# The entry of a two-layer transformer block: other banks, row buffers, matmul order and load order for the last modulation quarters

## The chip, the core and the metric

The kernel runs on one core of one Trainium2 chip. The core has five engines that run side by side and meet only through semaphores: TensorE (PE in the profile, its weight loads PEld), VectorE (DVE), ScalarE (ACT), GpSimd (POOL) and SyncE (SP), which here only issues DMAs. The time is the device time of one execution in microseconds (us), lower is better. Before the change it was 1694.29 us, the median of three executions (1693.81, 1694.29 and 1697.91).

## The reference

Layer 0 begins with an RMS norm of 512 latent and 256 context tokens, a scale and a shift of each of the 1024 features that come from a conditioning vector ("modulation"), and a projection into queries, keys and values. Only this entry is touched by the change.

```python
s_c, s_cc = silu(c), silu(c_ctx)
mx = s_c @ mod_w[l] + mod_b[l]              # 6*1024 values: shift, scale, gate, twice
shx1, scx1, gx1, shx2, scx2, gx2 = split(mx, 6)
hx = rms(x, norm_mix_w[l]) * (1.0 + scx1) + shx1
hc = rms(ctx, norm_mix_w[l]) * (1.0 + scc1) + shc1   # the same with s_cc
ax, ac = even_mixer(hx, hc, ev_w_in, ...)   # q, k, v = h @ ev_w_in, then attention
```

What follows (attention, output projection, a SwiGLU feed-forward, and layer 1 with differential attention) makes up most of the time and is unchanged.

## The kernel before

**Tiling.** All tokens stand in six tiles of 128: 4 and 5 are context, 0 to 3 latent. They are taken in the order 4, 5, 0, 1, 2, 3 (`CTX_FIRST`). The 1024 features are eight slices k = 0 to 7 of 128. The normalised tokens are turned (transposed) by PE into `xT`, features on the partitions (lines 1161 to 1172); `modulated(k)` (line 1182) then scales and shifts slice k on DVE, casts it on ACT into a high part and subtracts on DVE (latent) or POOL (context) into a low part. The tiles of these parts are hT0, hT1 for latent and hTc0, hTc1 for context tokens.

**Modulation.** Shift (part 0) and scale (part 1) are made in four quarters n = 0 to 3 of 256 features. Quarter n serves the slices k = 2n and 2n+1. One quarter of one part is a run of `mod_steps` (line 168):

- two loads of 512 KB each (line 177, tile `modw`, "pieces" in what follows), and for each piece four matmuls into a PSUM tile `mod` (line 182). The trace counts each fp32 matmul twice, so a piece is "x8" there;
- a copy on ACT into the row buffer `modr` (line 185);
- two small matmuls `modcol` that bring the row into columns (line 191), in a PSUM bank that is named by the argument `bank`;
- `add_mod` on DVE: `modc` (line 276), and for the scale also `aff` (line 280).

Quarters 0, 1 and 2 ran to their end in `start_mod` (line 1152), with `mod` in the wide score buffers (pool `p_sc`) and `modcol` in the banks acc0 (shift) and acc1 (scale). Quarter 3 was `late` (line 1174), and its `mod` itself was in acc0 and acc1. There was one row buffer `modr` for all of them.

**Weights.** `weights0` (line 481) brings the first head group's projection weights in four units of 384 KB (tile `wir`, three loads each, line 491), casts each on ACT to `wihi` (line 498) and subtracts on DVE to `wilo` (line 499). The unit u serves the slices 2u and 2u+1. All four were loaded behind the pieces of quarter 3. Pieces and weights of the start share six buffers of one tag (`start_tile`, line 1149), in turn; so a load waits until the matmuls have read what its buffer held. The two shift pieces of quarter 3 lie elsewhere (`raw_tile`).

**Order.** A scheduler places the instructions of each engine by its own estimate, and every engine runs its list in order: an instruction that waits holds up all that stand behind it. From line 1175 on PE's list is given by the order of the code (`manual_schedule`); other matmuls, those of the latent tokens above all, are filled in between by the scheduler. The projections are `inps` (line 465): tokens 4, 5, 0 and 1 collect in two wide score buffers, token 2 in acc0 and token 3 in acc1; 24 matmuls each. SP's list is one queue for all loads. `behind(name)` makes the scheduler place what is inside it after the instruction remembered under that name.

Of the kernel before, what the change touches and what calls it, by code (L numbers as in the profile page):

```python
# [63 lines left out]
def backbone(es: ExitStack, tc: tile.TileContext, x, c, ctx, c_ctx, mod_w, mod_b, norm_mix_w, norm_ffn_w,  # L64
# [3 lines left out]
    nc = tc.nc  # L68
# [7 lines left out]
    p_sc = None  # L76
    turn = {"acc": 0, "tr": 0, "sum": 0}
# [29 lines left out]
    @contextmanager  # L107
    def behind(*names):

        with ExitStack() as st:  # L110
            for name in names:
                if name in turn:
                    st.enter_context(tc.issue_after(turn[name].ins))
            yield

    def f32(ap):
        return ap.bitcast(F32)
# [4 lines left out]
    start = Pool("start")  # L122
# [45 lines left out]
    def mod_steps(l, part, n, new_tile, pool, bank, wide=None, room=("modr", 1)):  # L168

        width, pieces = 256, 2  # L170
        c0 = part * D + n * width
        ps = p_1.tile([P, width], F32, name="mod", tag=bank) if wide is None else \
            wide.pool.tile([P, 1024], F32, name="mod", tag="sc", bufs=2)[:, :width]
        kp = KT // pieces
        for pc in range(pieces):
            w = new_tile([P, kp, width], "modw")
            nc.sync.dma_start(
                w, mod_w[l, pc * kp * P:(pc + 1) * kp * P, c0:c0 + width].rearrange("(j p) n -> p j n", p=P))
            for a in range(kp):
                k = pc * kp + a  # L180
                j = k % 4
                nc.tensor.matmul(ps[32 * j:32 * j + 32, :], s_pad[:, k, :], w[:, a, :],
                                 start=k < 4, stop=k >= 4, tile_position=(0, 32 * j))
        r = pool.tile([P, width], F32, name="modr", tag=room[0], bufs=room[1])
        turn["modr"] = nc.scalar.copy(r, ps)
        yield
        nb = width // P
        k0, k1 = n * nb, (n + 1) * nb
        pc2 = p_1.tile([P, nb, 2], F32, name="modcol", tag=bank)
        for b in range(nb):  # L190
            nc.tensor.matmul(pc2[:, b, :], r[:, b * P:(b + 1) * P], sel2, start=True, stop=True)
        add_mod(l, part, k0, k1, pc2, 2)

    def mod_chunk(*args, **kw):
        for _ in mod_steps(*args, **kw):
            pass

    def mod_stream(groups, pool, bank):
# [74 lines left out]
    def add_mod(l, part, k0, k1, ps, streams):  # L273

        mc = modc[l][:, part, k0:k1, 0:streams]
        nc.vector.tensor_tensor(mc, ps, bc(bcol[:, l, part, k0:k1], 2, streams), ALU.add)
        if part in (1, 4):
            f = 0 if part == 1 else 1
            w0 = 16 + 16 * f + 8 * l
            nc.vector.scalar_tensor_tensor(aff[l][:, f, k0:k1, 0:streams], mc, 1.0,  # L280
                                           bc(cols[:, w0 + k0:w0 + k1], 2, streams), ALU.add, ALU.mult)
# [24 lines left out]
    def ctx_room(shape, dtype, name):  # L306

        return [keep.tile(shape, dtype, name=f"{name}{j}", tag=f"hTc{j}") for j in range(2)]
# [7 lines left out]
    def cols_T(j, s0, s1):  # L316

        return hT[j][0][:, :, s0:s1] if s1 <= SEQ else hT[j][1][:, :, s0 - SEQ:s1 - SEQ]
# [162 lines left out]
    def weights0(b, wp, subs, new_tile=raw_tile, loads=((0, 1), (), (2,), (3,))):  # L481

        qc, kc, vc = ((b * 256, 512 + 64 * b, 640 + 64 * b) if b < 2 else
                      (768 + (b - 2) * 256, 1280 + 64 * (b - 2), 1408 + 64 * (b - 2)))
        for u in range(4):
            if not u:
                raws = []
            for v in loads[u]:
                raws.append(new_tile([P, 2, 384], "wir"))
                for c0, c1, s in ((0, 256, qc), (256, 320, kc), (320, 384, vc)):  # L490
                    turn["load"] = nc.sync.dma_start(
                        raws[-1][:, :, c0:c1],
                        ev_w_in[0, v * 256:(v + 1) * 256, s:s + c1 - c0].rearrange("(j p) n -> p j n", p=P))
            if not u:
                yield
            raw = raws.pop(0)
            hi, lo = (wp.tile([P, 2, 384], F32R, name=f"wi{z}", tag=f"w{z}", bufs=WBUF + 1) for z in ("hi", "lo"))
            nc.scalar.copy(hi, raw)
            subs[u % len(subs)].tensor_sub(lo, raw, f32(hi))
            yield hi, lo  # L500
# [264 lines left out]
    def out_units0(wp):  # L765
        def tile(name, dtype):
            return wp.tile([P, D], dtype, name=name, tag="w", bufs=2 * KT)

        raws = [tile("wor", F32) if k < KT - 2 else raw_tile([P, D], "wor") for k in range(KT)]
        for k, raw in enumerate(raws):  # L770
            nc.sync.dma_start(raw, ev_w_out[0, k * P:(k + 1) * P, :])
        for raw in raws:
            hi, lo = tile("woh", F32R), tile("wol", F32R)
            nc.scalar.copy(hi, raw)
            nc.vector.tensor_sub(lo, raw, f32(hi))
            yield hi, lo
# [375 lines left out]
    def start_mod(n):  # L1152
        for part in range(2):
            mod_chunk(0, part, n, start_tile, start.pool, f"acc{part}", p_sc)

    p_sc = Pool("p_sc0", space=PSUM)
    wp = Pool("mw0", "right")
# [5 lines left out]
    for t in CTX_FIRST:  # L1163
# [4 lines left out]
        for g in range(2):  # L1168
# [1 line left out]
            for k in range(4):  # L1170
                nc.tensor.transpose(pt[:, k, :], h[:, (4 * g + k) * P:(4 * g + k + 1) * P], ident)
            nc.scalar.copy(xT[:, 4 * g:4 * g + 4, t * P:(t + 1) * P], pt)
    start_mod(2)
    late = [mod_steps(0, part, 3, (raw_tile, start_tile)[part], start.pool, f"acc{part}") for part in range(2)]
    manual = tc.manual_schedule(engines={mybir.EngineType.PE})
    manual.__enter__()
    for g in late:
        next(g)
    units = weights0(0, wp.pool, (nc.vector,), start_tile, ((0, 1, 2, 3), (), (), ()))
    next(units)  # L1180

    def modulated(k):
        for i, (s0, s1) in ((1, (SEQ, TOK)), (0, (0, SEQ))):
            nc.vector.tensor_scalar(xT[:, k, s0:s1], xT[:, k, s0:s1], aff[0][:, 0, k, i:i + 1],
                                    modc[0][:, 0, k, i:i + 1], ALU.mult, ALU.add)
        for s0, s1, ks in ((SEQ, TOK, slice(k - 1, k + 1)), (0, SEQ, slice(k, k + 1))):
            if s0 == 0 or k % 2:
                hi, lo = (cols_T(j, s0, s1)[:, ks, :] for j in range(2))
                turn["started"] = nc.scalar.copy(hi, xT[:, ks, s0:s1])
                (nc.gpsimd if s0 else nc.vector).tensor_sub(lo, xT[:, ks, s0:s1], f32(hi))  # L1190

    ws, begun, first = [], {}, CTX_FIRST[:2]
    for k in range(6):
        modulated(k)
        if k % 2:
            ws += islice(units, 1)
    for i in range(0, 4, 2):
# [88 lines left out]
    units = weights0(1, wp.pool, (nc.gpsimd, nc.vector))  # L1286
# [3 lines left out]
    if True:  # L1290
        for i, (b, t) in enumerate(steps):
# [8 lines left out]
            if j == 4 and b < 2:  # L1300
                units = weights0(b + 2, wp.pool, (nc.gpsimd, nc.vector))
# [28 lines left out]
            if t == 0:  # L1330
# [13 lines left out]
                wp = Pool("w0", "right")  # L1344
                opa = Pool("opa", "right")
                xs = [None] * NT
                units = out_units0(wp.pool)
# [17 lines left out]
            else:  # L1365
# [8 lines left out]
                if t == 4:  # L1374
                    room = [z[:, 0] for z in ctx_room([P, 1, KT, P], F32, "nroom")]
# [185 lines left out]
    p_sc = Pool("p_sc1", space=PSUM)  # L1561
    fp = out0
    mods1.close()
    wp = Pool("mw1", "right")
# [7 lines left out]
    late = []  # L1572
# [36 lines left out]
    if True:  # L1609
# [117 lines left out]
        wp = Pool("w1", "right")  # L1727
# [146 lines left out]
    p_sc = None  # L1874
# [56 lines left out]
```

## Time and profile before

| what | value |
|---|---|
| time, median of three | 1694.29 us |
| time, lowest and highest | 1693.81, 1697.91 us |
| span of the profiled execution, first to last instruction | 1695.6 us |
| PE busy | 1631.5 us, 96% of the span |
| DVE, ACT, POOL busy | 1146.7, 937.0, 696.4 us |
| mean granted TensorE clock | 0.992 |

The timed values are those of the three executions; of the profiled one the page tells the span, 1.3 us above the median. Times "at 42.91" are counted from the span's start. A row of a timeline gives the start, the length, the engine, the line, what it writes and reads, the count, and in brackets how long the engine had been idle and what released it. The entry of layer 0 are the first 45 of the 1695.6 us.

### The profile page before, as it was taken

How to read it: one execution, taken by the hardware profiler on the slowest of the kernel's cores; microseconds unless marked ns; L12 is line 12 of the kernel's file. 1: busy time of each engine (PE TensorE's matmuls, PEld its weight loads, DVE VectorE, ACT ScalarE, POOL GpSimd, SP SyncE). 2: the span in 40 equal slices, each digit the busy share in tenths (PEclk: the TensorE clock that was granted, in tenths of full speed). 3: DMA queues.
4: the chain of work that ended last, by engine and by line, in shares of the span. 5: the costliest groups of instructions: out<-in, count | busy, mean ns of one | idle time of the engine just before them, and what ended most of it. 6: DMA issues, size and time to landing. Idle time of an engine off the chain costs nothing. (4 is left out here: it accounts for less than half of the span.)

```text
span 1695.6 us, 28585 instructions
## 1 busy us (share of the span) xinstructions
PE 1631.5 (96%) x10390; PEld 1468.6 (87%) x10390; DVE 1146.7 (68%) x2014; ACT 937.0 (55%) x2011; POOL 696.4 (41%) x867
## 2 busy tenths in 40 slices
PE   6999999899999999999999989999999999999998
PEld 3977787677999999998777889999988899999887
DVE  3765656754799887767767656666666598887434
ACT  5565555745456665545554456666666555555320
POOL 2665554321346554412413366666664242221000
PEclk8999999999999999999999999999999999999999
DMA  9222221411455555439966311111112433331431
GB/s 319 69 71 74 70 70 50 164 60 38 129 167 172 164 159 162 134 108 347 296 184 189 99 43 38 48 42 44 50 45 97 125 93 102 111 101 57 137 99 62
DMA packets 218108, 194.64 MB, mean 115 GB/s; under 512 B 20016, under 2 KB 202864, under 8 KB 217968
## 3 DMA queue, kind: packets, MB, share of 16 engines
q1 hardware_dynamic: 217616, 192.62, 36.8%
q8 instruction: 81, 1.33, 0.3%
q14 instruction: 59, 0.48, 0.1%
q10 hardware_dynamic: 352, 0.21, 0.0%
HBM read 179.92 MB, written 12.87 MB: 114 GB/s over the span
## 5 line engine op out<-in xcount | busy, mean ns | idle before, releaser
L901 ACT CAST wbh<-wr 128x512 fp32r<-128x512 f32 x170 | 104.9, 621 | 130.2 <-PE p L933 73.4
L933 PE MATMUL p<-hT,wbh 128*128 128x256 f32 (+1 forms) x752 | 154.5, 299 | 0.0
L465 PE MATMUL inps<-wih,hT 128*128 128x384 f32 x512 | 144.2, 344 | 7.3 <-ACT qkv L677 7.3
L911 POOL TENSOR_TENSOR wbl<-wr,wbh 128x512 fp32r<-128x512 f32 x43 | 60.0, 1396 | 173.6 <-ACT wbh L901 173.6
L933 PEld LDWEIGHTS p<-hT,wbh 128*128 128x128 f32 x752 | 121.9, 191 | 0.2
L911 DVE TENSOR_TENSOR wbl<-wr,wbh 128x512 fp32r<-128x512 f32 x127 | 107.7, 858 | 21.0 <-ACT wbh L901 16.8
L933 PE MATMUL p<-hT,wbl 128*128 128x256 f32 (+1 forms) x376 | 111.9, 298 | 0.0
L933 PE MATMUL p<-t,wbh 128*128 128x384 f32 (+1 forms) x480 | 111.3, 318 | 0.0
L604 POOL TENSOR_SCALAR Pt<-Pt,rc 128x256 f32<-128x256 f32 (+3 forms) x96 | 74.6, 788 | 89.3 <-DVE rc L601 83.1
L231 POOL TENSOR_TENSOR modp<-modp 128x512 f32<-128x512 f32 x40 | 57.4, 1436 | 114.3 <-ACT modp L230 114.3
L465 PEld LDWEIGHTS inps<-wih,hT 128*128 128x128 f32 x512 | 93.3, 188 | 10.6 <-ACT qkv L677 9.7
L933 PE MATMUL p<-hTt,wbh 128*128 128x256 f32 (+1 forms) x480 | 101.0, 302 | 0.0
L887 POOL TENSOR_TENSOR wr<-wr 128x512 f32<-128x512 f32 x40 | 61.6, 1540 | 89.8 <-DVE ws L892 85.8
L933 PE MATMUL p<-b,wbh 128*128 128x384 f32 x368 | 93.8, 336 | 0.2 <-DVE c L961 0.2
L901 ACT CAST wbh<-ws 128x512 fp32r<-128x512 f32 x120 | 69.4, 579 | 43.1 <-PE p L933 29.0
L224 DVE SCALAR_TENSOR_TENSOR ma<-modw,cols,ma 128x256 f32<-128x256 f32 x140 | 89.2, 637 | 2.3
L592 ACT ACTIVATE Pt<-sc,nm 128x256 f32<-128x256 f32 (+3 forms) x96 | 67.6, 707 | 35.3 <-DVE nm L588 16.9
L465 PE MATMUL inps<-wil,hT 128*128 128x384 f32 x256 | 86.0, 336 | 0.0
L933 PEld LDWEIGHTS p<-t,wbh 128*128 128x128 f32 x480 | 82.9, 189 | 0.0
L911 DVE TENSOR_TENSOR wbl<-ws,wbh 128x512 fp32r<-128x512 f32 x120 | 81.7, 681 | 1.7 <-ACT wbh L901 1.6
L933 PEld LDWEIGHTS p<-hTt,wbh 128*128 128x128 f32 x480 | 78.3, 191 | 3.1 <-ACT modp L230 1.6
L230 ACT ACTIVATE modp<-modw,cols 128x256 f32<-128x256 f32 x160 | 68.4, 500 | 18.0 <-POOL ma L236 10.1
(355 smaller groups left out, 5217.9 us busy)
## 6 DMA issues: line engine op xcount, KB each, us to landing
modw<-in_mod_w_dram SPq DMA_DIRECT2D x96, 512.0 KB, 5.2
wr<-in_ffn_w_in_dram SPq DMA_DIRECT2D x176, 256.0 KB, 2.9
wdr<-in_ffn_w_out_dram SPq DMA_DIRECT2D x66, 512.0 KB, 3.7
wir<-in_od_w_in_dram SPq DMA_DIRECT2D x96, 128.0 KB, 2.3
hidm<-hid SPq DMA_DIRECT2D x44, 192.0 KB, 1.9
hr<-hidm SPq DMA_DIRECT2D x22, 192.0 KB, 3.5
x<-in_x_dram SPq DMA_DIRECT2D x8, 512.0 KB, 3.5
wir<-in_ev_w_in_dram SPq DMA_DIRECT2D x16, 256.0 KB, 3.5
```

The costliest lines, as they stand in the source:

```text
L224: nc.vector.scalar_tensor_tensor(acc, w[:, k], scale[k], acc, ALU.mult, ALU.add)
L230: nc.scalar.activation(pr[:, k], w[:, k], AF.Copy, scale=scale[k])
L231: nc.gpsimd.tensor_add(pr[:, 0:2], pr[:, 0:2], pr[:, 2:4])
L465: nc.tensor.matmul(ps, hs[j][:, k, :], ws[k // 2][z][:, k % 2, c0:c1], start=(k, j, z) == (0, 0, 0), stop=(k, j, z) == (KT - 1, 1, 0))
L592: turn["exp"] = nc.scalar.activation(p[:, :n], s, AF.Exp, bias=nm[:, c1], accum_out=sm[:, c1])
L604: nc.gpsimd.tensor_scalar(p[:, :n], p[:, :n], rc[:, hh:hh + 1], 1.0, ALU.mult, ALU.mult)
L887: nc.gpsimd.tensor_sub(w, raw[f, "G1"], w)
L901: nc.scalar.copy(hi, w)
L911: (nc.gpsimd if name == "G2" else nc.vector).tensor_sub(lo, raw[need[n]], f32(hi))
L933: nc.tensor.matmul(ps, w[:, k, :], H[b][h][:, k, :], start=first and k == 0 and q == 0, stop=final and k == 3 and q == 2, skip_group_check ...
```

## The change

Quarter 2 leaves `start_mod` and becomes `third`, which is stepped by hand like quarter 3. Quarter 3 (`late`) has its banks in tr0 and tr1, which the transposes of the tokens used until then. There are two row buffers `modr`. PE's given order now begins with quarter 2. The loads of weight unit 0 are issued between the shift pieces and the scale pieces of quarter 3, those of units 1 to 3 after them. DVE's and ACT's work on the slices k = 2 and up is placed behind the row copy of quarter 2.

```diff
     def mod_chunk(*args, **kw):
-        for _ in mod_steps(*args, **kw):
+        for _ in mod_steps(*args, room=("modr", 2), **kw):
             pass
...
-    start_mod(2)
-    late = [mod_steps(0, part, 3, (raw_tile, start_tile)[part], start.pool, f"acc{part}") for part in range(2)]
+    third = [mod_steps(0, part, 2, start_tile, start.pool, f"acc{part}", p_sc, ("modr", 2)) for part in range(2)]
+    late = [mod_steps(0, part, 3, (raw_tile, start_tile)[part], start.pool, f"tr{part}", None, ("modr", 2)) for part in range(2)]
     manual = tc.manual_schedule(engines={mybir.EngineType.PE})
     manual.__enter__()
-    for g in late:
+
+    def mods_end(g):
+        for _ in g:
+            pass
+
+    for g in third:
         next(g)
-    units = weights0(0, wp.pool, (nc.vector,), start_tile, ((0, 1, 2, 3), (), (), ()))
+    turn["third"] = turn["modr"]
+    mods_end(third[0])
+    next(late[0])
+    units = weights0(0, wp.pool, (nc.vector,), start_tile, ((0,), (1, 2, 3), (), ()))
     next(units)
+    mods_end(third[1])
+    next(late[1])
...
     for k in range(6):
-        modulated(k)
+        with behind(*(("third",) if k > 1 else ())):
+            modulated(k)
```

The new order on **PE**, from the last `modcol` of quarter 1 (the scale's) to the first projections. `mod` "x4" is one piece; `x12` are three pieces that follow each other; `inps` are projections, from context tokens where they read hTc and from latent ones where they read hT.

```order
 L191 MATMUL modcol<-cst,modr 128x2 x2
-L182 MATMUL mod<-modw,s_pad 32x256 x12
-L191 MATMUL modcol<-cst,modr 128x2 x2
-L182 MATMUL mod<-modw,s_pad 32x256 x12
+L182 MATMUL mod<-modw,s_pad 32x256 x16
 L191 MATMUL modcol<-cst,modr 128x2 x2
 L182 MATMUL mod<-modw,s_pad 32x256 x8
+L191 MATMUL modcol<-cst,modr 128x2 x2
+L182 MATMUL mod<-modw,s_pad 32x256 x4
+L465 MATMUL inps<-wihi,hT_110 128x384
+L182 MATMUL mod<-modw,s_pad 32x256 x4
 L465 MATMUL inps<-wihi,hTc_112 128x384
```

Before, PE ran three pieces of quarter 2, the shift's `modcol`, the last piece of quarter 2 with two of quarter 3, the scale's `modcol`, and two pieces. Now all four pieces of quarter 2 come first, then `modcol` (shift), the two shift pieces of quarter 3, `modcol` (scale), and the scale pieces of quarter 3 with one projection of token 2 between them.

On **SP**, the loads from the small head-weight row `rw` on; `wir` 128x2x256 and 128x2x64 x2 together are one weight unit.

```order
 L386 DMA rw<-in_ev_kn_a_dram 128x64
-L177 DMA modw<-in_mod_w_dram 128x4x256 x6
-L491 DMA wir<-in_ev_w_in_dram 128x2x256
-L491 DMA wir<-in_ev_w_in_dram 128x2x64 x2
+L177 DMA modw<-in_mod_w_dram 128x4x256 x4
+L491 DMA wir<-in_ev_w_in_dram 128x2x256
+L491 DMA wir<-in_ev_w_in_dram 128x2x64 x2
+L177 DMA modw<-in_mod_w_dram 128x4x256 x2
```

Weight unit 0 moved ahead of two pieces, the scale pieces of quarter 3. The shift pieces of quarter 3 had been issued further up in both, since their buffers are free from the start.

On **DVE**, before, from the subtractions of the latent slices k = 1 to 3 (`hT`) on: the two `modc` are quarter 2's shift and, with `aff`, its scale; `xT` is the modulation of k = 4.

```order
L1190 TENSOR_TENSOR hT_111<-xT,hT_110 128x512 x3
L276 TENSOR_TENSOR modc_106<-modcol,bcol 128x4 x2
L280 SCALAR_TENSOR_TENSOR aff_108<-modc_106,cols 128x4
L1184 TENSOR_SCALAR xT<-xT,aff_108,modc_106 128x256
L1184 TENSOR_SCALAR xT<-xT,aff_108,modc_106 128x512
```

And now, from the subtraction of k = 1 on; `wilo` is the subtraction of weight unit 0.

```order
L1200 TENSOR_TENSOR hT_111<-xT,hT_110 128x512
L276 TENSOR_TENSOR modc_106<-modcol,bcol 128x4
L1200 TENSOR_TENSOR hT_111<-xT,hT_110 128x512 x2
L499 TENSOR_TENSOR wilo<-wir,wihi 128x768
L276 TENSOR_TENSOR modc_106<-modcol,bcol 128x4
L280 SCALAR_TENSOR_TENSOR aff_108<-modc_106,cols 128x4
```

The shift's `modc` went up by two subtractions, and the scale's `modc`, on which the slices k = 4 and 5 wait, now stands behind `wilo` of unit 0. Behind this place the lists of PE, ACT, DVE and POOL differ in small swaps within the first attention blocks (the first 400 or so of some 8100 rows of PE's list) and are the same after that; SP's list differs only in what is shown.

## Prediction

> **What bounds the kernel now.** I read the page first, then the entry by stretches, then the timelines of PE, ACT, DVE and SP there.
>
> ```profile
> span 1695.6 us, 28585 instructions
> PE 1631.5 (96%) x10390; PEld 1468.6 (87%) x10390; DVE 1146.7 (68%) x2014; ACT 937.0 (55%) x2011; POOL 696.4 (41%) x867
> ...
> DMA  9222221411455555439966311111112433331431
> ```
>
> PE is busy 96% of the span, so nearly all of what is left to win on PE's idle time is 1695.6 - 1631.5 = 64 us, and the change reaches only the first 45 us of it. DMA is full (9) only in the first slice of 42 us and again in the middle.
>
> ```profile
> 20.00:30.00 10.00, 8.60 (x46) 6.31 (x47) 4.71 (x10) 6.33 (x14) 3.48 (x7) 0.52 1.10 347
> 30.00:40.00 10.00, 6.45 (x65) 3.56 (x64) 6.39 (x13) 4.77 (x10) 1.86 (x1) 0.84 1.07 311
> 40.00:50.00 10.00, 9.75 (x60) 8.39 (x61) 9.10 (x18) 5.23 (x9) 2.89 (x1) 0.79 0.37 111
> 60.00:70.00 10.00, 10.00 (x62) 9.89 (x60) 5.32 (x11) 3.98 (x10) 9.11 (x13) 1.00 0.15 42
> ```
>
> Columns: stretch, then busy us of PE, PEld, DVE, ACT, POOL, the granted clock, the DMA share and GB/s. Until 40 us the loads run at their full rate (share about 1.1, 347 GB/s); from 43 us on PE has no gap until 70. So the entry has two bounds in turn: the loads up to the last modulation piece, then PE. Between them lies what the change can win: the time from the landing of the last piece to the first projection. It is seen on PE:
>
> ```profile
> 31.47 1.07 PE L182 MATMUL mod<-modw,s_pad 128*32 128x256 f32 x16
> 33.20 0.64 PE L182 MATMUL mod<-modw,s_pad 128*32 128x256 f32 x8 [0.67 <-DMA modw<-in_mod_w_dram]
> 35.62 0.61 PE L191 MATMUL modcol<-cst,modr 128*128 128x2 f32 x4 [1.77 <-ACT modr L185]
> 36.15 0.64 PE L182 MATMUL mod<-modw,s_pad 128*32 128x256 f32 x8
> 37.91 1.94 PE L182 MATMUL mod<-modw,s_pad 128*32 128x256 f32 x16 [1.12 <-DVE modc L276]
> 39.77 1.02 PE L191 MATMUL modcol<-cst,modr 128*128 128x2 f32 x4
> 41.04 1.93 PE L182 MATMUL mod<-modw,s_pad 128*32 128x256 f32 x16 [0.25 <-DVE modc L276]
> 42.91 1.56 PE L465 MATMUL inps<-wihi,hTc 128*128 128x384 f32 x4
> ```
>
> The first projection starts at 42.91. Ahead of it stand quarter 2 (31.47, 33.20, 36.15) and the shift and scale pieces of quarter 3 (37.91, 41.04), and the waits there are on ACT's `modr` and DVE's `modc`, not on loads. When the last piece landed is told by SP:
>
> ```profile
> L177 SPq DMA_DIRECT2D modw<-in_mod_w_dram x1: 367/367/367, 29.8 to 29.8; - x1
> ...
> DMA to landing us min/median/max: 7.7/7.7/7.7
> ```
> ```profile
> L491 SPq DMA_DIRECT2D wir<-in_ev_w_in_dram x1: 367/367/367, 32.2 to 32.2; - x1
> ...
> DMA to landing us min/median/max: 6.2/6.2/6.2
> ```
>
> The last piece was issued at 29.8 and landed at 37.5, and PE took it at about 41.5. Four us of the entry are not the loads' fault. The first part of weight unit 0 landed at 38.4.
>
> **The change part by part.** The sum is made as a difference within this one profiled execution (span 1695.6) and taken off the median of the runs, 1694.3.
>
> *Banks and row buffers.* The rows that show what goes:
>
> ```profile
> 40.88 0.37 ACT L185 COPY modr<-mod 128x256 f32<-128x256 f32 x1 [3.60 <-PE modcol L191]
> ```
> ```profile
> 34.81 2.97 DVE L1190 TENSOR_TENSOR hT<-xT,hT 128x512 fp32r<-128x512 f32 x3
> 37.70 0.15 DVE L276 TENSOR_TENSOR modc<-modcol,bcol 128x4 f32<-128x4 f32 x1
> 40.83 0.16 DVE L276 TENSOR_TENSOR modc<-modcol,bcol 128x4 f32<-128x4 f32 x1 [2.97 <-PE modcol L191]
> ```
>
> At 37.91 the shift of quarter 3 wrote into acc0 and had to wait until DVE had read quarter 2's column out of it (37.70), and DVE came to that only after three subtractions (2.97 us). At 41.04 the same for acc1 and the scale (40.83). In tr0 and tr1 the last users are the tokens' transposes, which stand ahead of 31.47 in PE's list, so both waits go. ACT's copy at 40.88 waited for the one row buffer; with two it does not. That quarters 0 and 1 have the second buffer as well I price at nothing: their copies waited for `mod`, not for a buffer.
>
> *PE's order.* All of quarter 2 first, so the scale's last piece runs when it lands. Pieces of 512 KB at 347 GB/s land 1.5 us apart; the one two ahead of the last landed at 37.5 - 3.0 = 34.5. New times on PE, with the lengths of the rows above: last piece of quarter 2 at 34.6 to 35.3; shift's `modcol` (0.61) to 35.9; shift pieces of quarter 3, both landed long ago, 1.07 at full clock, to 37.0; scale's `modcol` to 37.6 (ACT has copied its row by 35.9).
>
> *The loads.* The total is the same, but 384 KB of weights now stand ahead of the two scale pieces: 1.1 us. So these land at about 37.1 and 38.6. The second takes the buffer of quarter 2's first piece, so SP issues it when weight unit 0 was issued before, at 32.2 instead of 29.8. The bounds from the two landing rows are 32.2 + 6.2 = 38.4 and 32.2 + 7.7 = 39.9; at 32.2 six us of loads are still queued, so I take 38.6. PE does the first scale piece to 38.2, then the one projection of token 2, which needs `wihi` of unit 0, then the second piece from 38.7 to 39.4. **The first regular projection starts at 39.5 instead of 42.9: 3.4 us.** With the upper landing it would be 40.7, 2.2 us.
>
> *Weights ahead.* Unit 0 lands at about 36. Its cast stands in ACT's queue behind the row copy of quarter 2's scale and three casts:
>
> ```profile
> 34.16 0.62 ACT L1189 CAST hT<-xT 128x512 fp32r<-128x512 f32 x1 [1.02 <-DVE xT L1184]
> 34.68 0.61 ACT L1189 CAST hTc<-xT 128x512 fp32r<-128x512 f32 x1
> 41.15 0.83 ACT L498 CAST wihi<-wir 128x768 fp32r<-128x768 f32 x1
> ```
>
> ACT's copy at 35.5, three casts at a distance of 0.5 each, the weight cast 37.3 to 38.1: in time for the projection at 38.2. The casts of slices 2 and 3 come 1.3 us later than before; nothing reads them before the projections of unit 1, some 3 us on.
>
> *What is late next.* The scale of quarter 2 now waits on DVE behind `wilo` of unit 0, and slices 4 to 7 follow:
>
> ```profile
> 41.02 0.16 DVE L280 SCALAR_TENSOR_TENSOR aff<-modc,cols 128x4 f32<-128x4 f32 x1
> 41.22 1.65 DVE L1184 TENSOR_SCALAR xT<-xT,aff,modc 128x256 f32<-128x256 f32 x4
> 42.79 0.95 DVE L499 TENSOR_TENSOR wilo<-wir,wihi 128x768 fp32r<-128x768 f32 x1
> ...
> 50.30 1.65 DVE L1184 TENSOR_SCALAR xT<-xT,aff,modc 128x256 f32<-128x256 f32 x4
> ```
>
> New on DVE: `wilo` of unit 0 to 39.2, `aff` 39.5, slices 4 and 5 by 41.1 (42.9 before: 1.8 earlier), then what filled the 7.5 us from 42.79 to 50.30 without the 0.9 for unit 0, so slices 6 and 7 begin at about 47.7 instead of 50.3. That is 2.6 us earlier, while PE comes 3.4 us earlier. Before, PE ran over this place without a gap; I charge nothing, or up to 1 us if PE catches up with them.
>
> *The clock.* PE's two `mod` rows of the same 16 matmuls took 1.07 and 1.94 us, and stretches of 3.41 us that fit the clock's steps tell when it drops:
>
> ```profile
> 30.58:33.99 3.41, 2.60 (x34) 1.48 (x32) 2.54 (x7) 2.21 (x4) 0.00 (x0) 1.00 1.10 348
> 33.99:37.41 3.42, 1.18 (x12) 0.68 (x12) 3.41 (x6) 2.30 (x5) 1.86 (x1) 1.00 1.13 327
> 37.41:40.82 3.41, 2.88 (x20) 1.53 (x20) 0.44 (x2) 0.00 (x0) 0.00 (x0) 0.50 0.91 232
> 40.82:44.23 3.41, 3.19 (x20) 1.92 (x21) 3.33 (x8) 3.21 (x6) 0.15 (x1) 0.50 0.78 240
> ...
> 846.37:849.78 3.41, 1.74 (x7) 0.92 (x6) 1.53 (x1) 2.25 (x4) 1.27 (x1) 1.00 0.75 220
> 849.78:853.19 3.41, 3.41 (x9) 2.66 (x9) 2.56 (x4) 1.17 (x2) 1.11 (x1) 0.50 0.75 219
> ```
>
> With 1.18 of 3.42 us busy (and 1.74 of 3.41, later) the clock was halved in the next stretch; with 2.60 it was not. With the new times PE is busy in 34.0 to 37.4 for 0.7 + 0.6 + 1.1 + 0.4 = 2.8 us: the clock stays full. Before, the projections from 42.91 to 44.23 ran at half, a loss of 0.66 us, which would go too. The Trainium skill ("TensorE: Matmul & The Clock Gate", section "What's actually happening") says that the clock drops after an idle window of some 3.4 us and returns after a busy one, and that the windows run free of the kernel. The rows agree on the length; they differ on the drop, since a stretch a third to a half busy was enough. As a rule about gaps it would give no drop in either kernel, and by it the entry's gain would be 3.4 without the clock's 0.7.
>
> *Sum.* 3.4 for the start, 0.7 for the clock, less up to 1 where PE catches up with slices 6 and 7: 2.7 to 4.1, and I take **3.3 us** for the entry. From there the lists of all engines hardly differ and the loads are not near their limit until the middle of the kernel, so an earlier entry should move the whole rest. In the first attention blocks small swaps add perhaps 1.5 us either way, as PE idles there:
>
> ```profile
> 75.00:100.00 25.00, 22.40 (x156) 19.16 (x155) 15.72 (x55) 16.31 (x51) 20.52 (x38) 1.00 0.14 47
> 100.00:125.00 25.00, 22.20 (x170) 17.04 (x168) 17.34 (x48) 16.26 (x44) 15.95 (x24) 1.00 0.27 75
> ```
>
> That is 2.6 + 2.8 = 5.4 us of idle time, which another order can shrink or stretch by a part. Forecast: 1694.3 - 3.3 = **1691.0 us**, 0.2%.
>
> **The rivals.**
>
> *The clock is low all the same.* If PE's wait for the scale piece falls so that a stretch is under half busy, the projections from 39.5 to 44.2 run at half clock and lose 2.35 us, against 0.66 before. Then the gain is 3.4 + 0.66 - 2.35 = 1.7: 1692.6 us. For it speaks that the stretches need not lie as in this execution, against it the 2.8 of 3.4 us. By the rows, 2.88 of 3.41 us busy did not bring the clock back and 3.19 did, so a lowered clock stays for a whole stretch or two. The Trainium skill says the same in that section, with one busy window as the condition.
>
> *The gain is given back in the first attention blocks.* PE waits there on DVE, ACT and POOL. If one of their lists is not moved forward by the entry, the 3.3 us turn into waits: 1694.3. Against it: in the entry DVE, the busiest of them (9.10 of 10 us), ends about as much earlier as PE.
>
> *The swaps in ACT's list make it slower.* In one place ACT's copy `qkv`, which frees a PSUM bank for the next projection, now stands behind the cast `qd`, and that cast can wait for POOL:
>
> ```profile
> 64.92 0.41 ACT L525 CAST qd<-qy 128x256 fp32r<-128x256 f32 x1 [3.93 <-POOL qy L523]
> 70.45 0.44 PE L465 MATMUL inps<-wihi,hTc 128*128 128x384 f32 x1 [0.23 <-ACT qkv L520]
> ```
>
> PE has waited only 0.23 for such a copy. If a copy stood behind a wait like the 3.93 and PE had nothing else, one costs 3.9 - 3.3 = 0.6 us more than the gain, two of them 4.5: 1694.9 to 1698.8, and I take 1696. It decides once these waits are over 3.3 us together.
>
> *The swaps fall well.* 3.3 from the entry and some 2 of the 5.4 us of idle time: 1689.
>
> **How the numbers follow.** Forecast 0.50, low clock 0.20, given back 0.12, slower 0.08, swaps well 0.10. The range leaves out the slower case and most of the last: 1688.8 to 1695.2. About 0.3%, 5.1 us, is what a measurement of this kernel tells from no change. Below 1689.2: half of the swaps that fall well and a tenth of the forecast's cases and some luck in the runs, 0.14. Above 1699.4: part of the slower case, 0.03. The rest, 0.83, is within.
>
> **What would show it.** In the new trace: no wait of `mod` on DVE `modc` for quarter 3; the last scale piece landing near 38.6 and taken at once; the first `inps` on context tokens near 39.5; granted clock 1.00 from 37 us on; slices 6 and 7 on DVE near 47.7; and every later stage about 3.3 us earlier. It is wrong if that last piece lands past 40, if `wihi` of unit 0 ends past 39, or if PE's idle time from 70 to 125 grows by what the entry gained.

## The result and the profile after

| | before | after |
|---|---|---|
| median of 20 executions each | 1696.00 us | 1698.71 us |
| lowest and highest | 1691.63, 1698.89 | 1693.74, 1702.97 |
| span of the profiled execution | 1695.6 | 1695.3 |
| mean granted clock in it | 0.992 | 0.995 |

The ratio after to before is 1.0019, with a 95% interval of 1.0011 to 1.0027: the change costs about 3.2 us by the ratio (the two medians differ by 2.7) where 3.3 were to be gained. The two profiled spans don't show it, since one execution scatters by more than that. The profiled execution of after took 1697.11 us, 1.8 above its span; by the same 1.8, an estimate, that of before took 1697.4, so the prediction was built on one of the slower executions of before. Where the time goes has to be read stage by stage. The page and the stretches of the kernel after, columns as before:

```profile
span 1695.3 us, 28585 instructions
...
PE 1631.9 (96%) x10390; PEld 1466.8 (87%) x10390; DVE 1145.2 (68%) x2014; ACT 937.2 (55%) x2011; POOL 696.8 (41%) x867
```
```profile
20.00:30.00 10.00, 7.37 (x72) 5.37 (x68) 5.91 (x12) 8.59 (x18) 3.65 (x7) 1.00 1.10 347
30.00:40.00 10.00, 6.58 (x52) 3.19 (x56) 5.98 (x13) 4.38 (x9) 1.32 (x1) 0.69 1.13 327
40.00:50.00 10.00, 10.00 (x59) 8.12 (x52) 9.86 (x23) 4.42 (x8) 4.30 (x1) 0.80 0.45 127
```

The sixth number is the clock. From 20 to 30 us it is 1.00 now (0.52 before), from 30 to 50 it is low. PE's timeline shows what that does:

```profile
30.83 0.64 PE L182 MATMUL mod<-modw,s_pad 128*32 128x256 f32 x8 [0.88 <-DMA modw<-in_mod_w_dram]
33.57 0.91 PE L182 MATMUL mod<-modw,s_pad 128*32 128x256 f32 x8 [2.10 <-DMA modw<-in_mod_w_dram]
34.97 1.08 PE L182 MATMUL mod<-modw,s_pad 128*32 128x256 f32 x8 [0.49 <-DMA modw<-in_mod_w_dram]
35.98 1.01 PE L191 MATMUL modcol<-cst,modr 128*128 128x2 f32 x4
36.93 1.93 PE L182 MATMUL mod<-modw,s_pad 128*32 128x256 f32 x16
38.79 1.01 PE L191 MATMUL modcol<-cst,modr 128*128 128x2 f32 x4
39.73 1.08 PE L182 MATMUL mod<-modw,s_pad 128*32 128x256 f32 x8
40.74 0.69 PE L465 MATMUL inps<-wihi,hT 128*128 128x384 f32 x1
41.36 1.08 PE L182 MATMUL mod<-modw,s_pad 128*32 128x256 f32 x8
42.38 1.65 PE L465 MATMUL inps<-wihi,hTc 128*128 128x384 f32 x4
```

The waits on DVE's `modc` are gone, as the change meant. But PE, done with the tokens' transposes at 29 us, waits 0.88 and 2.10 us for pieces; the same 16 matmuls then take 1.93 instead of 1.07 us, four small ones 1.01 instead of 0.61, and the first projection on context tokens starts at 42.38, not 39.5. In stretches that fit the clock's steps:

```profile
30.38:33.80 3.42, 0.87 (x13) 0.34 (x16) 2.96 (x7) 0.96 (x3) 0.00 (x0) 1.00 1.11 339
33.80:37.21 3.41, 2.92 (x24) 1.33 (x20) 0.17 (x2) 1.09 (x3) 0.00 (x0) 0.50 1.11 333
37.21:40.62 3.41, 3.41 (x28) 1.52 (x20) 3.09 (x5) 1.94 (x4) 1.32 (x1) 0.50 1.12 291
40.62:44.04 3.42, 3.42 (x18) 2.15 (x15) 3.39 (x7) 3.28 (x6) 1.27 (x1) 0.50 0.82 229
44.04:47.45 3.41, 3.41 (x22) 3.41 (x22) 3.41 (x7) 0.91 (x2) 3.02 (x1) 1.00 0.09 19
```

PE was busy for 0.87 us of one stretch, and three stretches of half clock follow, over the last modulation pieces and the first projections.

The second loss stands in the first attention blocks, on PE (first fence, after) and on ACT and POOL (second and third):

```profile
82.07 0.25 PE L543 MATMUL kpt<-identr,kd 128*128 128x128 f32 x1
83.66 0.28 PE L543 MATMUL kpt<-identr,kd 128*128 128x128 f32 x1 [1.34 <-POOL kd L530]
84.26 0.45 PE L465 MATMUL inps<-wihi,hT 128*128 128x384 f32 x1 [0.32 <-ACT qkv L520]
```
```profile
83.22 0.40 ACT L525 CAST qd<-qy 128x256 fp32r<-128x256 f32 x1 [1.64 <-POOL qy L523]
83.54 0.29 ACT L529 CAST kd<-qy 128x128 fp32r<-128x128 f32 x1
83.73 0.47 ACT L520 COPY qkv<-inps 128x384 f32<-128x384 f32 x1
```
```profile
81.28 1.22 POOL L160 TENSOR_TENSOR rs_q<-rs_q,neghalf 128x5 f32<-128x5 f32 x1
82.47 0.72 POOL L523 TENSOR_TENSOR qy<-qy,rs_q 128x320 f32<-128x320 f32 x1
83.15 0.45 POOL L530 TENSOR_TENSOR kd<-qy,kd 128x128 fp32r<-128x128 f32 x1
```

PE needs POOL's `kd` at 82.3, but in POOL's new list it stands behind the next token's `rs_q` and `qy`. ACT's `qkv`, which frees the bank for PE's next projection, stands behind the cast `qd`, which waits 1.64 us for the same `qy`. It stands behind `qd` in before's list too, and starts at 83.98 there; POOL's `qy` starts at 82.45. ACT's first `qkv` of all was 1.07 us earlier in after (57.33 against 58.40), so on the way to this place ACT and POOL have lost most or all of that, and PE, which was 1.34 us ahead at 80 us, has to wait. Before, PE's one wait shown from 79 to 86 us was 0.21. The gap is also followed by half clock; the stretches of after, then of before:

```profile
81.58:85.00 3.42, 1.76 (x12) 1.44 (x12) 1.85 (x7) 1.78 (x7) 3.42 (x6) 1.00 0.00 0
85.00:88.41 3.41, 3.41 (x13) 3.41 (x12) 1.98 (x5) 1.91 (x8) 2.91 (x6) 0.50 0.05 13
```
```profile
81.58:85.00 3.42, 3.07 (x23) 2.59 (x22) 2.17 (x9) 3.41 (x13) 3.25 (x6) 1.00 0.00 0
85.00:88.41 3.41, 3.41 (x22) 3.38 (x21) 1.73 (x8) 2.20 (x9) 3.23 (x8) 1.00 0.03 6
```

A fully busy stretch at half clock does half of its work: 3.41 / 2 = 1.7 us lost. It is not a loss on top of the waits, though. In the other profile of the same kernel, after_look below, the clock was full from 48 to 201 us: PE waited for `kd` as here (1.35 us), then 1.37 us at 92.59 for POOL's `Pt`, and from 60 to 140 us it lost 2.05 us, as much as after (2.07).

### The profile page after: what moved, and what is told of

Read it like the earlier page. It is cut to its first block, busy times and chain, and to the rows that moved or that the text cites. A ratio compares the mean times of both kernels' runs of the same rounds, so it can differ in the third digit from the quotient of the medians.

```text
span 1695.3 us, 28585 instructions
## 1 busy us (share of the span) xinstructions
PE 1631.9 (96%) x10390; PEld 1466.8 (87%) x10390; DVE 1145.2 (68%) x2014; ACT 937.2 (55%) x2011; POOL 696.8 (41%) x867
## 5 line engine op out<-in xcount | busy, mean ns | idle before, releaser
L901 ACT CAST wbh<-ws 128x512 fp32r<-128x512 f32 x120 | 69.4, 579 | 42.9 <-PE p L933 32.2
L465 PE MATMUL inps<-wihi,hT 128*128 128x384 f32 x256 | 77.1, 358 | 0.6 <-ACT qkv L520 0.3
```

The source lines that it names most:

```text
L465: nc.tensor.matmul(ps, hs[j][:, k, :], ws[k // 2][z][:, k % 2, c0:c1], start=(k, j, z) == (0, 0, 0), stop=(k, j, z) == (KT - 1, 1, 0))
L901: nc.scalar.copy(hi, w)
```

## The experiments

Times are the ratio to before measured beside it, with the 95% interval, then from each profile: where the clock was halved between 30 and 50 us, when the first context projection and ACT's first `qkv` copy start, and by how much PE's instructions lie behind (+) or ahead of (-) the same ones in before's profile at 60 and at 140 us. "Old" order of blocks means that ACT, DVE, POOL and PE do the first attention blocks in before's order. A shift is that of one execution, and does not stand for the ratio: behind 140 us the lists are before's but for a swap or two, and still a profile drifts by up to 5.7 us more, above all near 200 us and from 840 to 940.

| kernel | blocks | ratio (95%) | halved, us | context | `qkv` | shift at 60, 140 |
|---|---|---|---|---|---|---|
| before | old | 1 | 37.4 to 44.2 | 42.91 | 58.40 | 0, 0 |
| before_look | old | 1693.26 us, once | 33.3 to 43.5 | 41.96 | 57.56 | -0.84, -0.71 |
| after | new | 1.0019 (1.0011 to 1.0027) | 33.8 to 44.0 | 42.38 | 57.33 | -0.55, +1.52 |
| after_look | new | 1704.40 us, once | 34.2 to 47.9 | 42.10 | 58.96 | +1.08, +3.13 |
| new_entry_old_blocks | old | 1.0011 (1.0001 to 1.0022) | 32.5 to 46.1 | 42.01 | 58.10 | +0.22, +0.18 |
| old_entry_new_blocks | new | 1.0009 (1.0001 to 1.0018) | 32.6 to 42.8 | 41.22 | 56.84 | -1.56, +0.87 |
| rw_back | new, 1 move | 1.0017 (1.0003 to 1.0030) | 32.8 to 43.0 | 42.13 | 56.73 | -1.15, +0.87 |
| kd_back | new, 1 move | 1.0016 (1.0005 to 1.0028) | until 30.6 | 39.62 | 53.85 | -4.03, -1.42 |
| kd_and_qkv_back | new, 2 moves | 1.0037 (1.0023 to 1.0051) | 34.9 to 48.6 | 42.26 | 59.36 | +1.48, +4.48 |
| kd_qkv_rw_back | new, 3 moves | 1.0012 (0.9999 to 1.0025) | 32.9 to 43.1 | 42.04 | 56.73 | -1.15, -0.28 |
| banks_and_rows_only | old | 1.0031 (1.0019 to 1.0043) | 35.8 to 49.4 | 41.41 | 55.66 | +1.59, +0.46 |
| weights_not_ahead | old | 1.0010 (0.9998 to 1.0023) | until 31.1 | 40.56 | 55.15 | -1.52, -2.50 |
| old_entry_pe_busy | old | 0.9977 (0.9968 to 0.9987) | none | 40.50 | 54.04 | -2.80, -3.49 |
| new_entry_pe_busy | new | 1.0001 (0.9990 to 1.0011) | none | 40.55 | 56.84 | -3.12, +1.14 |
| new_entry_old_blocks_pe_busy | old | 0.9990 (0.9980 to 0.9999) | none | 40.18 | 56.47 | -3.49, -0.09 |
| new_entry_old_blocks_pe_busy_same_order | old | 0.9969 (0.9956 to 0.9981) | none | 40.29 | 54.69 | -3.19, -3.22 |

### Entry and blocks apart

Edges that only the scheduler sees were added, so that each engine's list in the first attention blocks follows a table (`LOCK`, one row of instruction numbers an engine). With the new entry the table is before's order, with the old entry after's:

```diff
+            if i == 13:
+                made_by = {int(z.name[2:]) - base: z for z in traced[mark:]}
+                for order in LOCK:
+                    for z0, z1 in zip(order, order[1:]):
+                        tc.add_manual_dep(made_by[z1], made_by[z0].name, mybir.DependencyInfo(
+                            mybir.DependencyClass.NoSync, mybir.DependencyReason.DATA), reason="lock")
```

> The changed entry, with the order of ACT, DVE, POOL and PE in the first attention blocks (57 to 140 us) pinned to that of before. Theory S (the swaps in those blocks lose what the entry gains, and more): PE's list is about 1 us ahead of before at 57 us and stays 1 to 2 us ahead at 140, the granted clock is full from 60 to 140 us, and the time is 1 to 2 us below before, 3 to 4 us below the changed kernel. Theory E (the entry itself costs, by halved clock or by loads, and the swaps are neutral): the time is that of the changed kernel, 2 to 3 us above before. Theory N (nothing but chance in the clock's steps): the same as before within 1 us.

> The entry of before, with the order in the first attention blocks pinned to that of the changed kernel: the other half of the cross. Theory S: 3 to 4 us above before, with PE's list 2 to 3 us behind at 140 us, and new waits of PE near 84 us. Theory E: like before. Theory N: within 1 us of before.

Neither theory S (the first kernel 1 to 2 us below before, the second 3 to 4 above) nor theory N came. Each half of the change costs by itself: 0.0011 x 1695.7 = 1.9 us the entry, 1.5 us the order of the blocks, together about the 3.2 measured; both intervals begin at 1.0001, only just clear of no change. The shift columns show the second half cleanly: in the two kernels PE's lead changes by -0.04 us from 60 to 140 with the old order and by +2.43 with the new. The first is not seen there in one execution, and became the question of the clock.

### Single moves in the first blocks

The changed kernel, its own order pinned, with one DVE instruction (1392 is `rw`, 445 `qd`, 412 `sm`, 414 `rc`) or one on POOL (243 is `kd`, 437 and 438 are `rs_q`, 297 is `qy`) moved; then both POOL's and ACT's (548 is `qkv`, 299 the waiting `qd`, 302 its `kd`); then all three.

```diff
 DVE, rw_back
-553, 1392, 445, 412, 414, 456
+553, 445, 412, 414, 1392, 456
 POOL, kd_back
-369, 437, 438, 297, 243, 374
+369, 243, 437, 438, 297, 374
 ACT, kd_and_qkv_back (with POOL's move)
-267, 299, 302, 548, 310
+267, 548, 299, 302, 310
```

> The changed kernel with one DVE instruction moved: the scaling of the row rw of the second table (L387), which waits for a DMA, back behind the three instructions qd, sm and rc that stood ahead of it before. Theory S1 (this wait is what costs, since rc lets POOL's softmax scaling and then PE's ppt go): DVE no longer waits 2.5 us ahead of rc, PE's ppt comes 1 to 2 us earlier than in the changed kernel from 90 us on, the time is 1 to 2 us below the changed kernel. Theory S2 (another swap costs): within 0.5 us of the changed kernel.

> The changed kernel with one POOL instruction moved: the subtraction kd of one token (L530) back ahead of the next token's rsqrt and scaling. Theory S2 (PE's wait of 1.3 us for kd at 83.7 us, and the halved clock that follows it, cost): the wait of kpt on POOL kd is gone, no halved clock at 85 us, the time is 1.3 to 2.7 us below the changed kernel. Theory S1: within 0.5 us of the changed kernel, since PE then waits for the qkv copy or for ppt instead.

> The changed kernel with two instructions of the first attention blocks moved at 80 to 84 us: POOL's subtraction kd (L530) of a token ahead of the next token's rsqrt and scaling, and ACT's copy qkv (L520) ahead of the cast qd (L525) that waits for POOL. Theory 'two queues': the single move of kd left PE waiting 2.24 us for qkv, so both queues hold PE at the same place; with both moved PE waits there under 0.6 us, the clock is not halved at 82 to 88 us, the shift between 80 and 88 us is under 0.8 instead of 2.2 to 2.7, and the time falls by 1 to 2 us to about 1697. Rival 'chain': the token's work on POOL and DVE is itself too slow there, PE waits as long at the next step, and the time stays at 1698.5.

> The changed kernel with three instructions of the first attention blocks moved: POOL's kd ahead of the next token's rsqrt, ACT's qkv ahead of the waiting qd, and DVE's rw (L387) behind qd, sm and rc. With the first two PE passed 82 us without a wait, and then waited 2.97 us for POOL's Pt behind DVE's rw and its load. Theory 'three queues': with all three PE has no wait over 1 us between 80 and 100 us, the shift against before stays within 0.8 us from 80 to 100 and within 1.2 at 140, and the time is that of the new entry with the old block order, 1 to 2 us under the changed kernel. Rival 'chain': PE waits 2 us or more at some next step, and the time is within 0.7 us of the changed kernel's or above.

PE's longest wait from 79.5 to 98 us in kd_back, in kd_and_qkv_back and in kd_qkv_rw_back (line numbers are 7 higher with the table):

```profile
81.34 0.44 PE L472 MATMUL inps<-wihi,hT 128*128 128x384 f32 x1 [2.24 <-ACT qkv L527]
```
```profile
92.85 1.14 PE L619 MATMUL ppt<-cst,Pt 128*128 128x128 f32 x4 [2.97 <-POOL Pt L611]
```
```profile
88.89 0.90 PE L619 MATMUL ppt<-cst,Pt 128*128 128x128 f32 x4 [1.64 <-POOL Pt L611]
```

Each move did what it should at its place, and the wait came back at the next queue. With `kd` ahead, PE waited for `qkv` behind `qd`. With both ahead PE passed 82 us without a wait and stood 2.97 us for POOL's `Pt`, which needed DVE's `rc`, which stood behind `rw` and its load:

```profile
91.42 0.20 DVE L394 TENSOR_SCALAR rw<-rw 128x64 f32<-128x64 f32 x1 [2.52 <-DMA rw<-in_ev_qn_b_dram]
91.52 0.42 DVE L533 TENSOR_TENSOR qd<-qy,qd 128x256 fp32r<-128x256 f32 x1
91.86 0.15 DVE L606 TENSOR_TENSOR sm<-sm,es 128x2 f32<-128x2 f32 x1
92.05 0.17 DVE L608 RECIPROCAL rc<-sm 128x2 f32<-128x2 f32 x1
```

With all three, `Pt` stood behind another `rs_q` and `kd` on POOL (1.64 us). The shift from 60 to 140 is +2.61, +3.00 and +0.87 for the three, so together the moves take back more than half of the loss of 2.0 to 2.4, and one or two of them nothing. "Three queues" is right in direction; that no wait over 1 us would be left was wrong. In time no gain can be told: one move gave 1.0017 and 1.0016, two moves 1.0037 and three 1.0012, against 1.0019 for the changed kernel, and all four intervals overlap with its own.

### Keeping PE busy at the entry

While PE waits for pieces it transposes the identity into the unused half of a wide score buffer; nothing reads that. The counts stand ahead of the pieces of quarter 2's shift and scale and quarter 3's shift and scale.

```diff
+WARM = ((0, 7), (17, 4), (0, 0), (3, 3))
...
+            for _ in range(warm[pc]):
+                nc.tensor.transpose(turn["wide"][:, 512:640], ident, ident)
```

For old_entry_pe_busy the counts are ((0, 7), (7, 4), (8, 0), (8, 0)), in before's entry.

> The changed kernel, its own order everywhere, with 34 extra transposes of the identity into the unused half of the wide score buffer while PE waits for the modulation pieces (7 ahead of the second piece of quarter 2's shift, 17 and 4 ahead of the two pieces of its scale, 3 and 3 ahead of quarter 3's scale). Theory 'clock': the new entry lost because PE, faster up to 29 us and then idle for loads, had its clock halved from about 33 to 44 us; kept busy, it shows no half-clock stretch between 30 and 46 us and the first projection on context at 39.6 +-0.5 instead of 42.4, and the time falls by 1 to 2.5 us against the changed kernel, to about 1696.5 or 1 us above before. Rival 'loads': the first projection waits for the scale's last piece and the weights ahead of it whatever the clock; then it stays at 41 or later and the time at 1698.5. Rival 'work added': the extra transposes delay PE and the time rises by up to 3.6 us.

> The same extra transposes in the kernel with the new entry and the order of before in the first attention blocks. If the two losses are the halved clock at the entry and the order of the first blocks, this is the entry gain as predicted: 1692.5 to 1694.5, 1 to 3 us under before, with the first projection on context at 39.6 and no half-clock stretch at 82 to 88 us. If the blocks take back whatever PE gains ahead of them, it is within 0.5 us of before.

> Control: before, its own order, with extra transposes in its waits for pieces and for DVE (14 ahead of quarter 2's scale pieces, 4 ahead of the last of them, 8 ahead of quarter 3's shift and 8 ahead of its scale). Theory 'clock': before too loses some of its entry to half clock in part of its executions (its profile was halved again at 37.4 us), so keeping PE busy gives 0 to 1 us, and the first projection on context stands at 41 to 42.5 instead of 42.9. If it gains as much as the changed kernel does, the extra transposes, not the new entry, are what counts; if the changed kernel gains 1 us more, the new entry is better once the clock is full.

> As new_entry_old_blocks_pe_busy, with the other matmuls of the entry pinned in the order of the changed kernel: there 90 instead of 78 projection matmuls stood ahead of ACT's first qkv copy, 12 x 0.173 = 2.1 us. Theory 'first qkv copy': with 78 it falls from 56.5 to 54.4 us, and the time from 1692.1 (1.8 under before) to 3.5 to 4 us under before, level with the old entry kept busy. Rival: the slices 6 and 7 on DVE (48.3 us against 46.4 in the old entry kept busy) set the first qkv copy, which stays over 55.5, and the time stays 1.5 to 2.5 us under before.

PE in old_entry_pe_busy and then in the last of the four:

```profile
37.32 1.07 PE L196 MATMUL mod<-modw,s_pad 128*32 128x256 f32 x16
38.32 1.09 PE L192 MATMUL mod<-cst 128*128 128x128 f32 x8
39.34 1.07 PE L196 MATMUL mod<-modw,s_pad 128*32 128x256 f32 x16
40.50 0.97 PE L479 MATMUL inps<-wihi,hTc 128*128 128x384 f32 x4
```
```profile
36.58 1.07 PE L197 MATMUL mod<-modw,s_pad 128*32 128x256 f32 x16
37.58 0.61 PE L206 MATMUL modcol<-cst,modr 128*128 128x2 f32 x4
...
38.50 0.64 PE L197 MATMUL mod<-modw,s_pad 128*32 128x256 f32 x8
...
39.72 0.64 PE L197 MATMUL mod<-modw,s_pad 128*32 128x256 f32 x8
40.29 0.97 PE L480 MATMUL inps<-wihi,hTc 128*128 128x384 f32 x4
```

No half clock is left between 30 and 50 us, and 34 useless matmuls make the kernel faster: 0.0023 x 1693.9 = 3.9 us for the old entry, 0.0031 x 1695.9 = 5.3 us for the new one with the old block order, against before; their intervals overlap. The timed executions had a mean clock of 0.998 and 0.999 against 0.995 for before beside them; at the 0.9 to 1.1 us for 0.001 that goes with the executions of before, that is about 3 of the 3.9 us and 4 of the 5.3. The control therefore decides: most of what pays is the full clock, which the old entry can have as well. At full clock the two entries start the context projections at 40.50 and 40.29, so by these two profiles the entry itself is worth about 0.2 us. The times say less: the two kernels differ by 0.0008, or 1.4 us, and with these intervals anything from some -1.3 to 4 us (an estimate) is left open.

The two kernels with the new entry and no pinned order there gained less, and a fault of the edit explains it. With the transposes the scheduler put 42 instead of 30 latent projections ahead of ACT's first `qkv` copy, which stood at 56.8 and 56.5 us instead of 54.7 (12 x 0.173 = 2.1 expected). Until then PE was busy, but with matmuls that nobody waited for; the attention chain started late, and PE lost 1.74 us waiting for it at 69 us. With the order pinned the copy came at 54.69, and the time fell to 5.3 us under before, more than the 3.5 to 4 expected. The control has such a difference too, which nobody pinned: 24 latent projections stand ahead of that copy in old_entry_pe_busy and 33 in before, so some of its 3.9 us may be this order. "Slices 6 and 7" as the bound falls: they stood at 48.56, and the copy still at 54.69.

### Once more, and parts of the entry

before_look and after_look are the two kernels unchanged, in another execution. The other two have the old block order and a part of the change: only the banks tr0, tr1 and the row buffers; or all but the loads.

```diff
 banks_and_rows_only, against before
-(raw_tile, start_tile)[part], start.pool, f"acc{part}")
+(raw_tile, start_tile)[part], start.pool, f"tr{part}", None, ("modr", 2))
 weights_not_ahead, against after
-    units = weights0(0, wp.pool, (nc.vector,), start_tile, ((0,), (1, 2, 3), (), ()))
-    next(units)
     mods_end(third[1])
     next(late[1])
+    units = weights0(0, wp.pool, (nc.vector,), start_tile, ((0, 1, 2, 3), (), (), ()))
+    next(units)
```

> The kernel before once more. Theory 'clock': the new entry kept busy starts its context projections only 0.3 us ahead of the old one kept busy, so most of the 3.4 us that before's profile showed were its own halved clock (37.4 to 44.2 us) and not the bank waits; another execution, with the half clock elsewhere, starts them 1 to 2 us earlier, at 41 to 42, and ACT's first qkv copy at 56.5 to 57.5 instead of 58.4. If it is at 42.9 and 58.4 again, the profile was typical and this theory falls.

> The changed kernel once more: with the clock halved from about 33 to 44 us, context projections at 42 to 42.5 and first qkv copy at 56.7 to 59.4 as in four of its five relatives; or, with the early half clock, 39.6 and 53.9 as in one.

> Before with only the banks tr0 and tr1 for quarter 3 and two row buffers; loads as before, the order of the first attention blocks as before. The shift pieces of quarter 3 run at once, so PE's work there stands earlier and PE idles longer for the scale's last piece. Theory 'clock': the waits on DVE go, the clock is halved from about 33 us for three stretches all the same, and the first context projection stays at 41 to 42, bounded by the weights of unit 0; time within 1 us of before. If the banks are what costs (longer idle, four halved stretches), it is 1 to 2 us slower, first qkv copy at 58 to 59; if the waits were what bound the entry it is 1.5 to 3 us faster.

> The changed kernel with all of the first weights loaded behind the last modulation pieces again (banks, row buffers and PE's order as changed), and the order of the first attention blocks as before. Its neighbour with weights ahead was 1.9 us above before. If the weights ahead cost it (scale pieces 1.1 us later, DVE's slices 4 to 7 behind wilo, so longer idle and four halved stretches), this one is within 0.7 us of before, with slices 4 and 5 on DVE at 37 to 39.5 us instead of 40.3; if PE's order from quarter 2 on or the banks cost it, it stays 1.5 to 2 us above.

before_look starts the context projections at 41.96, 0.95 us earlier than the profile on which the prediction was built. PE in banks_and_rows_only, and the stretches there:

```profile
36.29 2.19 PE L189 MATMUL mod<-modw,s_pad 128*32 128x256 f32 x16
41.41 1.65 PE L472 MATMUL inps<-wihi,hTc 128*128 128x384 f32 x4 [2.93 <-ACT wihi L505]
```
```profile
35.75:39.17 3.42, 2.71 (x20) 0.93 (x19) 2.83 (x11) 1.48 (x4) 0.26 (x1) 0.50 1.13 324
39.17:42.58 3.41, 1.17 (x4) 1.17 (x5) 3.01 (x5) 2.06 (x4) 2.96 (x1) 0.50 0.93 233
42.58:45.99 3.41, 3.41 (x15) 3.41 (x14) 3.33 (x9) 1.56 (x3) 0.00 (x0) 0.50 0.75 204
45.99:49.41 3.42, 3.42 (x13) 3.42 (x12) 3.08 (x7) 3.22 (x6) 2.11 (x1) 0.50 0.09 15
```

The several short waits on DVE became one wait of 2.93 us for the weights of unit 0, and the clock stayed halved over four stretches, to 49.4 us. The first context projection stands at 41.41, within the 41.2 to 42.9 of the old entry at a halved clock, and the kernel is 0.0031 x 1695.7 = 5.3 us slower than before. So removing the bank waits alone did not pay. Why it costs is not shown: in the profile PE is only 0.46 us behind before at 140 us, and two thirds of the 4.8 us between the two spans arise behind 840 us, where the lists are the same. Nor did the edit change the banks and rows alone. The scheduler issued the 256 KB load of `rp` at 30.65, ahead of weight unit 0, instead of at 40.39, and put 8 instead of 33 latent projections ahead of ACT's first `qkv`. weights_not_ahead was to be within 0.7 us of before or 1.5 to 2 above; by its ratio it is 1.7 above with an interval of -0.3 to +3.9, which tells nothing, and its slices 4 and 5 came at 41.42, not at 37 to 39.5.

## Why the prediction was wrong

**The waits on DVE and the load order** went as predicted: no `mod` waits for `modc`. kd_back, whose changes lie at 80 us and whose entry is the changed one, happened to run with full clock from 30.6 us until 81.8, after half clock from 20.4 to 30.6:

```profile
39.05 0.64 PE L189 MATMUL mod<-modw,s_pad 128*32 128x256 f32 x8 [0.50 <-DMA modw<-in_mod_w_dram]
39.62 0.97 PE L472 MATMUL inps<-wihi,hTc 128*128 128x384 f32 x4
```

The last piece is taken as it lands at 39.05 (38.6 predicted, bounds 38.4 to 39.9), and the context projections start at 39.62 (39.5). Slices 6 and 7 began at 48.14 there and at 48.86 in after (47.7). With a full clock these steps hold, in one profile whose clock was full by luck.

**"The clock stays full"** is the first step that failed. It counted PE's work in 34.0 to 37.4 (2.8 us; 2.92 in the nearest stretch of after) and took the stretch ahead from before's profile, where PE was still busy with the transposes. They were late there because the clock had been at 0.52 from 20 to 30 us. In after it was 1.00, PE finished at 29 and idled into 33.8. The change is not needed for that: in before_look the clock was full up to 26.4 us, and halved from 33.3 to 43.5. The rival "the clock is low all the same" came, with a chance of 0.20, but its price counted half clock from 39.5 to 44.2 only. Measured was 33.8 to 44.0, and the projections started 2.9 us later than forecast.

**The gain itself** was mis-sized for the same reason. The 3.4 us were 42.91 - 39.5, a start at half clock against one at full clock. Like with like it is 40.50 - 40.29 = 0.2 us with PE busy (0.9 if kd_back's 39.62 is set against the 40.50, though only one of them has the transposes), and 41.2 to 42.9 against 42.0 to 42.4 with a halved clock. The rows of waits on `modc` named the right releaser, but most of the time behind them was the clock's. The sum has a slip besides: 3.4 + 0.7 - 1 is 3.1, not the 2.7 given as its lower end.

**"Small swaps ... 1.5 us either way", charged nothing**, is the second step that failed. The new order cost 1.5 us in timed runs, and 2.0 to 2.4 in the shift of after, after_look, old_entry_new_blocks and rw_back, always with one sign. The rival on ACT's list, a `qkv` put behind a `qd` that waits for POOL, did not come as it was told. That copy, at 72.59 in after, stands behind a `qd` that waited 0.77 us, and PE did not wait for it. What held PE was POOL's list, `kd` behind `rs_q` and `qy` (1.34 us) or later `Pt` (1.37 in after_look), and with `kd` moved ahead ACT's and DVE's lists in turn. Nearer was the rival that the gain is given back in these blocks, with a chance of 0.12: PE's lead went into waits on engines that had not come forward as far. But it was the new order that did this; with the old one and PE kept busy a lead of 3.2 us was still 3.2 at 140.

**"Every later stage about 3.3 us earlier"** followed from these two and fell with them.

**Still open** is why the new entry, with the old blocks, loses 1.9 us in timed runs. Its executions had a mean clock of 0.99364 against 0.99440 for before beside it, and one halved stretch is 0.5 x 3.41 / 1695 = 0.001 of it, so about 0.8 stretches more. At 0.9 us for 0.001 that is 0.7 of the 1.9 us; the rest has no explanation here. Four-stretch halvings were seen at the entry in three of seven profiles with the full new entry and no added transposes, and in none of three with the old one. But over the first 50 us both have three to five halved stretches in all, so the profiles do not show that the new entry has more. Where the half clock lay in the timed runs was not recorded.

## What to carry to other kernels

Before a wait is removed, ask what the clock makes of the idle time that is left: here the clock was halved just where PE becomes the bound, with the change and without it. Compare a start at full clock with a start at full clock, and take the state of one profile for what it is; a second profile of the kernel before would have shown 0.95 us of the gain to be chance. And pin the order of later stages when an edit ahead of them is tried: here the scheduler's new order there cost as much as the edit, and moving back one instruction showed nothing, since the next queue held PE at the same time.

## What was not expected of the hardware

The clock was halved after a stretch of 3.41 us in which PE was not idle but busy for 0.87 or 1.76 us. The busy time alone does not decide it: in after, the stretch from 23.55 to 26.97 had 1.70 us, and the clock stayed full. Its return was uneven: one fully busy stretch brought it back at 88.41, while at 44.04 and 49.41 it took two (2.92 us busy in 3.41 did not count). In 35 executions of before (1691.7 to 1699.4 us) the time falls as the mean granted clock rises, with a correlation of -0.77 and 0.9 us for 0.001, that is for one halved stretch; so a good part of the scatter between executions of one program goes with the number of its halved stretches. And the kernel with the lowest ratio here is one that does more: with 34 matmuls that nothing reads, 0.9969 (0.9956 to 0.9981) of the time before.
